# One layer of a hybrid encoder: the DeltaNet scan's q-k matrices as full 128x128 blocks, one product a step, and scratch buffers shared anew

## The chip, the cores and the metric

The kernel runs on one core of a Trainium2 chip. The metric is the time in microseconds (us) of one launch on that core; of several runs the median is taken, and the profile is of one execution. The core has engines that each work through a queue of their own, strictly in order: TensorE (PE: matrix products; PEld loads the stationary operand), VectorE (DVE), ScalarE (ACT), GpSimd (POOL) and SyncE (SP, which issues most transfers). Data lies in SBUF, products land in banks of PSUM, and semaphores make one engine wait for another.

## The reference, cut to what matters

768 tokens (one prompt of 256, one sample of 512), width 1024. The layer computes a modulated norm, one input projection, two mixers side by side (neighbourhood attention with 8 heads of 64; a gated DeltaNet in both directions with 4 heads of 128), one output projection, and a gated feed-forward part with a short convolution. The change is in the DeltaNet scan and in the norm of the attention's queries and keys:

```python
def _gated_delta_chunked(q, k, v, g, beta):          # CHUNK = 64
    ...
    a_mat = lower + jnp.eye(CHUNK, dtype=lower.dtype)
    u = lax.linalg.triangular_solve(a_mat, v * beta[..., None], ...)
    w = lax.linalg.triangular_solve(a_mat, kb * jnp.exp(gc)[..., None], ...)
    intra = jnp.where(causal, jnp.einsum('bhncd,bhnsd->bhncs', q, k) * decay, 0.0)
    ...
    def step(S, xs):
        q_i, k_i, u_i, w_i, a_i, gl_i = xs           # a_i is intra, the q-k matrix of a chunk
        v_new = u_i - jnp.einsum('bhcd,bhde->bhce', w_i, S)
        o = jnp.einsum('bhcd,bhde->bhce', q_i, S) + jnp.einsum('bhcs,bhse->bhce', a_i, v_new)
        S = S * jnp.exp(gl_i)[..., None, None] + jnp.einsum('bhcd,bhce->bhde', k_i, v_new)
        return S, o
...
    aq = _rmsnorm(aq.reshape(B, T, N_ATT_HEADS, ATT_HD), att_q_norm)
    ak = _rmsnorm(ak.reshape(B, T, N_ATT_HEADS, ATT_HD), att_k_norm)
```

## The kernel before, in words

**Tiling.** Weights and activations of the large projections are split into a high and a low half (hi, lo) and multiplied in three products (hi by hi, lo by hi, hi by lo); a projection is a long row of such products that depend on nothing but loaded weights. The DeltaNet's own products are plain 32-bit ones, each of which the trace shows as two instructions.

**The DeltaNet, by pairs of heads.** For each of two pairs (0 and 1) the stages are: `dn_proj` (q, k, v of the pair), `dn_decay`, `dn_scales`, `dn_gram` (the Gram products and from them `Ic`, the q-k matrices), `dn_solve` (the inverse of the triangular matrix of every chunk, a chain of small DVE and PE operations), `dn_scan`, and `dn_final` (squares on ACT L830, a Newton rsqrt of eleven small DVE operations L155 to L160 and L831, scaling on ACT L837, transposes on PE L842, gating on DVE L845, a store).

**A scan step.** A step handles one chunk of the forward direction in one half of the 128 partitions and one of the backward direction in the other. A scan has 24 steps: four rounds with both sequences and both heads of the pair (16 steps), and then four rounds with the sample alone (8 steps, two heads abreast). One step runs through this chain: the products of state and keys and queries (L768), `r` on DVE (two halves, L774) and `tm` on ACT (two halves, L781), the product with the inverse (L782), its scaled copies `XS` on DVE and ACT (L786, L788), two 64x128 copies into `XB` on ACT (L790), the products for the new state (L793), the state on DVE (two, L796), and the q-k products. `XB` holds each direction's rows with zeros in the other half, and two products with a 64-column operand (L802) give the two halves of the result, to which DVE adds `tm` (L806). The three groups of products of a step land in one PSUM bank. The state of the next step needs L796, so the rounds of one head and sequence follow each other.

**After a scan.** L818 adds the directions, and `dn_final` follows. After the second pair come the attention's blocks: `att_qk` projects 256 columns of queries or keys of half the heads (`att_proj`, L868), copies them to `raw` (L878), takes 24 squares with row sums on ACT into a throw-away tile `jk` (L884), forms the rsqrt on DVE (L885 and L155 to L160), multiplies (L888), and transposes on PE (L894). `att_v` projects the values, `att_core` does scores, softmax and mixing (first products at L944). The modulation vectors of the second norm are computed along the way (`ada`, L192).

**What sets the order.** The program text is not the order in which an engine works. A scheduler places the instructions of each engine; it may pull later, independent work, above all the projections, in between the steps of a scan. It can't pull a piece of work ahead of the last user of a buffer that it needs: every tile has a tag in a pool with a number of buffers, and the tiles of one tag take the buffers in turn, in the order of the program text. In the kernel before, `raw`, `jk` (tag `jka`), `s_` and `f_` of `att_qk` are in a pool `at` of their own, and `dn_final`'s `jk` is in the pool `dn` of the DeltaNet.

Of the kernel before, what the change touches and what calls it, by code (L numbers as in the profile page):

```python
# [17 lines left out]
P = 128  # L18
T = 768
D = 1024  # L20
# [25 lines left out]
NV1 = VEC["n1g"][0]  # L46
NC1 = CST["bo"][0]
# [55 lines left out]
def layer(ctx: ExitStack, tc: tile.TileContext, I: dict, yout: bass.AP, dbg=None):  # L103
# [7 lines left out]
    vec = cpool.tile([P, VEC["_n"][1] - NV1], F32, name="vec")  # L111
# [3 lines left out]
    nc.sync.dma_start(vec[:], I["vec"][:, NV1:])  # L115
    nc.scalar.dma_start(cst[:], I["cst"][:, NC2:])

    vec2 = []

    def V(n, i=0, m=None):  # L120
        o, w = VEC[n]
        t_, o = (vec, o - NV1) if o >= NV1 else (vec2[0], o)
        return t_[:, o + i:o + (i + m if m is not None else w)]
# [14 lines left out]
    def load_w(pool, src, bufs, hp=HPW):  # L138
        """[128, 1024] weights -> (hi, lo)"""
# [11 lines left out]
    def rsqrt(out, v, shape, tag):  # L151
        """out = v ** -0.5 (v > 0), Newton on the integer seed"""
        a = small.tile(shape, F32, name="rs_a", tag="rs_a" + tag, bufs=2)
        ti = small.tile(shape, I32, name="rs_t", tag="rs_t" + tag, bufs=2)
# [23 lines left out]
    bw = cpool.tile([P, KD, 32], F32R, name="bw")  # L178
    braw = arow[:, 0:128].rearrange("p (k c) -> p k c", k=KD)
    nc.scalar.dma_start(braw, I["wba"])  # L180
    split(braw, bw[:, :, 0:16], bw[:, :, 16:32])

# [4 lines left out]
    def ada_piece(s, i, row, brow, load, PS, w4=None):  # L187
        """rows k = 4 i.. of set s; the four partial sums in rows 32 k.."""
# [26 lines left out]
    def ada_ahead(sets, row, bias, load, PS):  # L215
        """each piece is loaded a step before it is used"""
# [24 lines left out]
    # ================= mixer =================  # L241
    with ExitStack() as mx:
# [20 lines left out]
        with tc.tile_pool(name="st", bufs=1, reuse_waits="tile") as st:  # L263
# [13 lines left out]
            # x, features on partitions  # L277
# [7 lines left out]
            # rstd of the tokens, along the free axis  # L285
# [50 lines left out]
            # the first four products run along with the rows of h  # L336
# [32 lines left out]
        at = px.enter_context(tc.tile_pool(name="at", bufs=1, side="right", reuse_waits="tile"))  # L369
# [14 lines left out]
        def gates_dn():  # L384
# [13 lines left out]
            ba = dn.tile([P, NT, 16], F32, name="ba")  # L398
# [3 lines left out]
            def to_slots(dst, src):  # L402
                """src [P, t, (d h)] -> dst [P, h, t', d]"""
# [10 lines left out]
            beta = dn.tile([P, 4, NT, 2], F32, name="beta")  # L414
            to_slots(beta, e1[:])
            y1 = dn.tile(sc8, F32, name="y1")
            nc.vector.tensor_tensor(y1[:], ba[:, :, 8:16], V("dtb").unsqueeze(1).broadcast_to(sc8), ALU.add)
            y2 = dn.tile(sc8, F32, name="y2")
# [4 lines left out]
            na = dn.tile([P, 8], F32, name="na")  # L423
            nc.scalar.activation(na[:], V("alog"), AF.Exp)
            nc.vector.scalar_tensor_tensor(y1[:], y1[:], -1.0, na[:].unsqueeze(1).broadcast_to(sc8), ALU.mult, ALU.mult)
            gg = dn.tile([P, 4, NT, 2], F32, name="gg")
# [16 lines left out]
            pdec = dn.tile(s48, F32, name="pdec")  # L443
# [40 lines left out]
        def ada_bufs():  # L484
            """buffers that the heads have left: five for weights, one for the bias row"""
# [3 lines left out]
            for tag, shape in (("dec", [P, 24, 64]), ("MO", [P, 12, P])):  # L489
                a_ = dn.tile(shape, F32, name="au", tag=tag)[:].rearrange("p a b -> p (a b)")  # L490
                raws.append(a_[:, 0:1024].rearrange("p (k c) -> p k c", k=2))
# [4 lines left out]
        def ada_load(src):  # L496
            """four k of a set"""
# [85 lines left out]
        def dn_scales(hp, sqs):  # L583
            # sums of squares: natural for k, swapped halves for q
# [6 lines left out]
            rkk = dn.tile([P, 2, NT], F32, name="rkk", tag="rkk", bufs=2)  # L591
# [782 lines left out]
```

## Time and profile before

| what | value |
|---|---|
| runs | 1201.08, 1195.68, 1190.89 us; median 1195.68 |
| span of the profiled execution | 1191.6 us |
| PE busy | 1150.3 us, 97% of the span |
| DVE / ACT / POOL busy | 726.8 us (61%) / 539.0 us (45%) / 69.0 us (6%) |
| scan of pair 0 | about 196 to 277 us of the span |
| solve of pair 1 | about 277 to 326 us |
| scan of pair 1 | about 326 to 407 us |
| first scores of the attention (L944) | 438.0 us |

The page gives no time around the span, so the profiled execution's own time is taken as its span; it lies 4.1 us, 0.3%, below the median of the runs and beside the fastest of them. A busy engine isn't one that sets the pace everywhere: what a stage is worth is read from that stage. In a row of a group, "x48 | 12.4, 259 | 2.3 <-PE" reads: 48 instructions, 12.4 us busy in all, 259 ns each in the mean, 2.3 us in which the engine stood idle before them, mostly waiting for PE.

### The profile page before, as it was taken

How to read it: one execution, taken by the hardware profiler on the slowest of the kernel's cores; microseconds unless marked ns; L12 is line 12 of the kernel's file. 1: busy time of each engine (PE TensorE's matmuls, PEld its weight loads, DVE VectorE, ACT ScalarE, POOL GpSimd, SP SyncE). 2: the span in 40 equal slices, each digit the busy share in tenths (PEclk: the TensorE clock that was granted, in tenths of full speed). 3: DMA queues.
4: the chain of work that ended last, by engine and by line, in shares of the span. 5: the costliest groups of instructions: out<-in, count | busy, mean ns of one | idle time of the engine just before them, and what ended most of it. 6: DMA issues, size and time to landing. Idle time of an engine off the chain costs nothing.

```text
span 1191.6 us, 17540 instructions
## 1 busy us (share of the span) xinstructions
PE 1150.3 (97%) x6682; PEld 940.3 (79%) x6682; DVE 726.8 (61%) x1544; ACT 539.0 (45%) x1301; POOL 69.0 (6%) x112
## 2 busy tenths in 40 slices
PE   6999899998999999999889999999999999999998
PEld 3778767777978698867678888888888888888886
DVE  5636986878476545364597655555655555564556
ACT  4357664574658666563476421430341233043310
POOL 1102103001100100100031000000000000000000
PEclk8999999999899999989999999999999999999999
DMA  8421142124241562281123411320311231031002
GB/s 306 197 71 36 54 142 90 58 94 142 73 149 55 176 231 72 76 264 60 59 75 106 142 54 29 113 66 6 115 63 36 71 89 53 18 102 58 19 1 106
DMA packets 43891, 110.98 MB, mean 93 GB/s; under 512 B 4384, under 2 KB 14528, under 8 KB 42528
## 3 DMA queue, kind: packets, MB, share of 16 engines
q1 hardware_dynamic: 36640, 92.93, 24.1%
q0 software_dynamic: 2928, 10.50, 2.7%
q10 hardware_dynamic: 4240, 6.44, 1.5%
q8 instruction: 52, 0.85, 0.3%
q14 instruction: 31, 0.25, 0.1%
HBM read 100.41 MB, written 9.45 MB: 92 GB/s over the span
## 4 chain that ended last, share of the span: by engine, by line
PE 79%; DVE 9%; ACT 7%; DMA 2%; issue 2%; SPq 0%; POOL 0%; DVEq 0%; ACTq 0%
PE dpt L1250 14%; PE upp L1169 10%; PE pjt L476 5%; PE pjt L868 4%; PE pat L1086 3%; PE sht L192 2%; PE pjt L345 2%; PE sdt L768 2%; ACT jk L884 1%; PE sdt L345 1%; PE sdt L944 1%; PE sdt L793 1%; PE sdt L802 1%; PE sdt L708 1%; PE mxt L970 1%
## 5 line engine op out<-in xcount | busy, mean ns | idle before, releaser
L136 DVE TENSOR_TENSOR wlo<-wraw,whi 128x1024 fp32r<-128x1024 f32 x72 | 88.1, 1223 | 115.9 <-ACT whi L135 115.7
L135 ACT CAST whi<-wraw 128x1024 fp32r<-128x1024 f32 x72 | 75.5, 1048 | 149.6 <-PE upp L1169 112.3
L1250 PE MATMUL dpt<-dh,gh 128*128 128x512 f32 x264 | 104.1, 395 | 0.2 <-DVE arow L1252 0.2
L1250 PE MATMUL dpt<-dl,gh 128*128 128x512 f32 x264 | 102.8, 389 | 0.0
L1250 PE MATMUL dpt<-dh,gl 128*128 128x512 f32 x264 | 102.3, 390 | 0.0
L1169 PE MATMUL upp<-h2lo,whi 128*128 128x256 f32 x352 | 99.8, 283 | 0.0
L1169 PE MATMUL upp<-h2hi,whi 128*128 128x256 f32 x352 | 98.8, 281 | 0.0
L1169 PE MATMUL upp<-h2hi,wlo 128*128 128x256 f32 x352 | 98.2, 279 | 0.0
L135 ACT CAST dh<-draw 128x1024 fp32r<-128x1024 f32 x22 | 23.1, 1052 | 160.4 <-PE dpt L1250 111.7
L1252 DVE TENSOR_TENSOR arow<-dpt,gb 128x512 f32<-128x512 f32 x72 | 49.8, 691 | 61.7 <-PE dpt L1250 59.6
L868 PE MATMUL pjt<-whi,hhi 128*128 128x256 f32 x288 | 85.4, 296 | 0.0
L868 PE MATMUL pjt<-whi,hlo 128*128 128x256 f32 x288 | 84.7, 294 | 0.0
L868 PE MATMUL pjt<-wlo,hhi 128*128 128x256 f32 x288 | 84.2, 292 | 0.0
L476 PE MATMUL pjt<-hhi,whi 128*128 128x512 f32 (+1 forms) x192 | 67.6, 352 | 1.3 <-DVE u L531 1.3
L476 PE MATMUL pjt<-hhi,wlo 128*128 128x512 f32 (+1 forms) x192 | 67.5, 353 | 0.0
L476 PE MATMUL pjt<-hlo,whi 128*128 128x512 f32 (+1 forms) x192 | 67.5, 352 | 0.0
L1169 PEld LDWEIGHTS upp<-h2hi,wlo 128*128 128x128 f32 x352 | 66.8, 190 | 0.2
L1169 PEld LDWEIGHTS upp<-h2hi,whi 128*128 128x128 f32 x352 | 66.3, 188 | 0.4
L1169 PEld LDWEIGHTS upp<-h2lo,whi 128*128 128x128 f32 x352 | 66.5, 189 | 0.0
L1250 PEld LDWEIGHTS dpt<-dh,gh 128*128 128x128 f32 x264 | 49.6, 188 | 13.4 <-DVE arow L1252 3.6
L868 PEld LDWEIGHTS pjt<-whi,hhi 128*128 128x128 f32 x288 | 55.9, 194 | 4.4 <-issue 3.6
L868 PEld LDWEIGHTS pjt<-whi,hlo 128*128 128x128 f32 x288 | 56.0, 195 | 2.5 <-issue 2.5
(910 smaller groups left out, 2882.7 us busy)
## 6 DMA issues: line engine op xcount, KB each, us to landing
wraw<-wup SPq DMA_DIRECT2D x44, 512.0 KB, 3.6
draw<-wdown SPq DMA_DIRECT2D x22, 512.0 KB, 3.5
araw<-ada SPq DMA_DIRECT2D x8, 1024.0 KB, 11.8
wraw<-wdn SPq DMA_DIRECT2D x16, 512.0 KB, 3.6
ew<-ada_w SPq DMA_DIRECT2D x16, 512.0 KB, 4.5
wraw<-wat SPq DMA_DIRECT2D x12, 512.0 KB, 4.1
sc<-abias POOLq DMA_DIRECT2D x24, 256.0 KB, 3.0
aw<-ada_w SPq DMA_DIRECT2D x10, 512.0 KB, 5.3
```

Source lines behind the costliest of these rows:

```text
L135: nc.scalar.copy(hi, src)
L136: nc.vector.tensor_tensor(lo, src, hi.bitcast(F32), ALU.subtract)
L192: nc.tensor.matmul(p_[32 * kk:32 * kk + 32, :], cs[:, 4 * i + kk, :], w4[kk], start=True, stop=True)
L345: nc.tensor.matmul(o_, w0[i][w][:, k * P:(k + 1) * P], m[:, k, c0:c1], start=(k == 0 and n == 0 and (c0 > 0 or i % 2 == 0)), stop=(k == KD ...
L476: nc.tensor.matmul(o_, w[:, k * P:(k + 1) * P], m[:, k, c0:c1], start=(k == 0 and n == 0), stop=(k == KD - 1 and n == 2))
L708: nc.tensor.matmul(ps[:, n * 32:n * 32 + 32], M16[:, n, :], R[:, n, :], start=True, stop=True)
L768: nc.tensor.matmul(ps1[:, d * P:(d + 1) * P], KQ[:, j, tl[d], 2 * pr[d]:2 * pr[d] + 2, :].rearrange("p b c -> p (b c)"), St[:, d, :], star ...
L868: nc.tensor.matmul(o_, a[:, k, t * P:(t + 1) * P], w[kh][m][:, kk * 256:(kk + 1) * 256], start=(k == 0 and n == 0 and t % 2 == 0), stop=(k ...
L1086: nc.tensor.matmul(pt[:], m[:, a, j, :], w[:, sl], start=(j == 0 and n == 0), stop=(j == len(ks) - 1 and n == 2))
L1169: nc.tensor.matmul(o_, (lo if n == 2 else hi)[:, k * P:(k + 1) * P], (h2lo if n == 1 else h2hi)[:, k, c0:c1], start=(k == 0 and n == 0), s ...
L1250: nc.tensor.matmul(ps[:], a[:, t * P:(t + 1) * P], m[:, sl], start=(i == 0 and n == 0), stop=(i == len(gs) - 1 and n == 2))
L1252: nc.vector.tensor_tensor(arow[:], ps[:], gb[:, grp(t), sl], ALU.mult)
```

## The change

**The q-k matrices.** `Ic` holds a full 128x128 block for every chunk instead of a 128x64 one. It is cleared on POOL, and the Gram stage writes each direction's 64x64 piece off the diagonal. `XB` and its clearing go. After the product with the inverse, ACT copies the whole 128x128 result once, back into `r` (which gets four buffers instead of two), and one product `Ic` by `r` gives both halves.

**The buffers.** `Ic` is larger by 12 KB a partition in two buffers, and other buffers are merged: the pool `at` goes. `rd` of `dn_decay`, which was in `at`, takes the tag `MO` of the solve. The attention's raw queries and keys lie in the second half of a buffer of tag `Ic` (`rest[0]`), whose first half holds the scores; both buffers are allocated before `att_half(0)`. `s_` and `f_` take the tags `beta` and `pdec`. The squares' throw-away tile `jk` of `att_qk` takes the tag `jk`, one buffer, which is also that of `dn_final`. The four states are one tile. Further small tiles share tags, three vectors at the end of `vec` are loaded later, by a POOL transfer in the output projection's phase, and some weights of the output projection are loaded into `rest[1]`.

```diff
-        XB = dn.tile([P, 2, 2, P], F32, name="XB", tag="XB")
-        nc.gpsimd.memset(XB[:], 0.0)
...
-            rd = at.tile([P, 24, 64], F32, name="rd", tag="raw")
+            rd = dn.tile([P, 24, 64], F32, name="rd", tag="MO")
...
-            Ic = dn.tile([P, 2, NT, 2, 64], F32, name="Ic", tag="Ic", bufs=2)
+            Ic = dn.tile([P, 2, NT, 2, P], F32, name="Ic", tag="Ic", bufs=2)
+            nc.gpsimd.memset(Ic[:].rearrange("p h t x c -> p (h t x c)"), 0.0)
...
-                            nc.vector.tensor_tensor(Ic[r_, j, b:b + n, e if d == 0 else 1 - e, :],
+                            nc.vector.tensor_tensor(Ic[r_, j, b:b + n, e if d == 0 else 1 - e, (1 - e) * 64:(1 - e) * 64 + 64],
...
-                r = dn.tile([P, P], F32, name="r", tag="r", bufs=2)
+                r = dn.tile([P, P], F32, name="r", tag="r", bufs=4)
...
-                for e in range(2):
-                    nc.scalar.copy(xb[half(e), e, :], ps2[half(e)])
+                nc.scalar.copy(r[:], ps2)
...
-                for e in range(2):
-                    nc.tensor.matmul(ps4[half(1 - e)], Ic[:, j, tp, x, :], xb[:, e, :], start=True, stop=True)
+                nc.tensor.matmul(ps4, Ic[:, j, tp, x, :], r[:], start=True, stop=True)
...
-            raw = at.tile([P, NT, 4, 64], F32, name="raw", tag="raw", bufs=1)
+            raw = rest[0].rearrange("p (t h c) -> p t h c", t=NT, h=4)
...
-            s_ = at.tile([P, 24], F32, name="s_", tag="s_")
-            f_ = at.tile([P, 24], F32, name="f_", tag="f_")
+            s_ = dn.tile([P, 24], F32, name="s_", tag="beta")
+            f_ = dn.tile([P, 24], F32, name="f_", tag="pdec")
             for i in range(24):
-                jk = at.tile([P, 64], F32, name="jk", tag="jka", bufs=1)
+                jk = dn.tile([P, 64], F32, name="jk", tag="jk", bufs=1)
                 nc.scalar.activation(jk[:], raw[:, i // 4, i % 4, :], AF.Square, accum_out=s_[:, i:i + 1])
...
+        scs, rest = [], []
+        for i in range(2):
+            sc3 = dn.tile([P, 6, 512], F32, name="sc", tag="Ic", bufs=2)
+            scs.extend(sc3[:, u] for u in range(3))
+            rest.append(sc3[:, 3:6].rearrange("p a b -> p (a b)"))
...
-                raw = wo.tile([P, D], F32, name="wraw", tag="wraw", bufs=WRB)[:]
+                raw = wo.tile([P, D], F32, name="wraw", tag="wraw")[:] if i % 2 else rest[1][:, 0:D]
...
+        vec3.append(fp.tile([P, VEC["_n"][1] - NV2], F32, name="vec3"))
+        nc.gpsimd.dma_start(vec3[0][:], I["vec"][:, NV2:])
```

**How the order changes.** In the changed file the lines carry slightly other numbers: its L769, L783, L801, L841, L867, L883, L893 and L191 are L768, L782, L802, L842, L868, L884, L894 and L192 of before. On PE, the last rounds of the second pair's scan in the kernel before: `pjt` is a projection's PSUM tile, `au`, `aw` and `arow` are operands of the modulation, `sdt` the scan's tile.

```order
L768 MATMUL sdt<-S_2915,KQ 128x128
L192 MATMUL sht<-au,cs 32x512 x3
L192 MATMUL sht<-aw,cs 32x512
L782 MATMUL sdt<-r,Wbd 128x128
L192 MATMUL sht<-aw,cs 32x512 x3
L868 MATMUL pjt<-whi,hhi 128x256
L868 MATMUL pjt<-whi,hlo 128x256
L868 MATMUL pjt<-wlo,hhi 128x256
L782 MATMUL sdt<-r,Wbd 128x128
L802 MATMUL sdt<-XB,Ic 64x128 x2
```

The same place in the changed kernel, up to the first projection after the scan:

```order
L769 MATMUL sdt<-S,KQ 128x128
L801 MATMUL sdt<-r,Ic 128x128
L769 MATMUL sdt<-S,KQ 128x128 x2
L783 MATMUL sdt<-r,Wbd 128x128 x2
L801 MATMUL sdt<-r,Ic 128x128 x2
L841 MATMUL sdt<-cst,Vt 128x128 x12
L893 MATMUL sht<-cst,sc 128x128 x12
L191 MATMUL sht<-aw,cs 32x512 x6
L191 MATMUL sht<-au,cs 32x512 x2
L867 MATMUL pjt<-whi,hhi 128x256
```

Projection and modulation products no longer stand between these rounds. In the changed kernel this holds for the last 15 of the scan's 24 steps, and the twelve transposes of `dn_final` (L841) and the first twelve of the raw queries (L893) stand ahead of the next projection product; in the kernel before the transposes L842 stand one by one between L868's.

On ACT, in the middle of the second pair's scan in the kernel before; the squares of the raw keys (into `s__3911`) stand between the scan's copies:

```order
L884 ACTIVATE jk,s__3911<-raw 128x64 x2
L790 COPY XB<-sdt 64x128 x2
L781 ACTIVATE tm<-sdt,egcs 64x128 x2
L830 ACTIVATE jk,so<-Vt 128x128
L884 ACTIVATE jk,s__3911<-raw 128x64
```

On ACT, at the end of the same scan in the changed kernel:

```order
L782 ACTIVATE tm<-sdt,egcs 64x128 x4
L790 COPY r<-sdt 128x128 x2
L829 ACTIVATE jk,so<-Vt 128x128 x10
L883 ACTIVATE jk,s__3524<-sc 128x64 x7
L836 ACTIVATE Vt<-Vt,fo 128x128 x11
L846 DMA mixn_73<-zz 128x768
L836 ACTIVATE Vt<-Vt,fo 128x128
L883 ACTIVATE jk,s__3524<-sc 128x64 x4
L846 DMA mixn_73<-zz 128x768
L883 ACTIVATE jk,s__3524<-sc 128x64 x13
```

All 24 squares of the first raw queries (`s__3524`) now stand behind the whole scan and behind `dn_final`'s squares (L829), two of which stand within the scan; in the kernel before all but one of the queries' squares stand ahead of the second pair's scan.

More of the change, by code (lines that the diff above doesn't have):

```diff
@@ L488, in ada_bufs @@
             raws.extend(w_[:, i] for i in range(3))
-            for tag, shape in (("dec", [P, 24, 64]), ("MO", [P, 12, P])):
-                a_ = dn.tile(shape, F32, name="au", tag=tag)[:].rearrange("p a b -> p (a b)")
+            for tag in ("dec", "MO"):
+                a_ = dn.tile([P, 1536], F32, name="au", tag=tag)
                 raws.append(a_[:, 0:1024].rearrange("p (k c) -> p k c", k=2))
@@ L747, in dn_scan @@
         def dn_scan(hp, KQ, Kt, Vt, pex, Ic, Wbd):
-            S = [[dn.tile([P, 2, P], F32, name=f"S{s}{j}", tag=f"S{s}{j}") for j in range(2)] for s in range(2)]
+            S_ = dn.tile([P, 4, 2, P], F32, name="S", tag="S")
+            S = [[S_[:, 2 * s + j] for j in range(2)] for s in range(2)]
             half = lambda e: slice(e * 64, e * 64 + 64)
@@ L886, in att_qk @@
             rsqrt(f_[:], s_[:], [P, 24], "24")
-            r3 = raw[:].rearrange("p t h c -> p (t h) c")
+            r3 = rest[0].rearrange("p (n c) -> p n c", c=64)
             nc.vector.tensor_tensor(r3, r3, f_[:].unsqueeze(2).broadcast_to([P, 24, 64]), ALU.mult)
@@ L1031, in layer @@
         att_half(0, iter(()), (0, 0, 0))
-        pTs = [dn.tile([P, 512], F32, name="pT", tag=t)[:] for t in ("XS", "XB")]
-        scs = []
-        for _ in range(2):
-            sc3 = dn.tile([P, 3, 512], F32, name="sc", tag="Ic", bufs=2)
-            scs.extend(sc3[:, u] for u in range(3))
+        pTs = [dn.tile([P, 512], F32, name="pT", tag=t)[:] for t in ("XS", "S")]
         core = att_core(0, QT[0], SD, SD, [(a, b, u) for a in range(2) for b in range(2) for u in range(3)])
@@ L1203, in out_proj @@
                 if t > 1:
-                    raw = wo.tile([P, KD, P], F32, name="mraw", tag="wraw", bufs=WRB)
+                    raw = (wo, wm)[t % 2].tile([P, KD, P], F32, name="mraw", tag="wraw")
                     m_ = wm.tile([P, 2, KD, P], F32R, name="m_", tag="m_", bufs=2)
```

43 lines of the change are left out of this document (21 added, 22 removed).

## The prediction

> **What bounds the kernel now.** First the page's head and its chain of waits, which say what the whole is limited by.
>
> ```profile
> span 1191.6 us, 17540 instructions
> PE 1150.3 (97%) x6682; PEld 940.3 (79%) x6682; DVE 726.8 (61%) x1544; ACT 539.0 (45%) x1301; POOL 69.0 (6%) x112
> PE 79%; DVE 9%; ACT 7%; DMA 2%; issue 2%; SPq 0%; POOL 0%; DVEq 0%; ACTq 0%
> ```
>
> PE is busy for 97% of the span and carries 79% of the chain that ends last. So an instruction taken off PE is worth its time there, and time in which PE stands still is lost in full, unless the span has such time already. The second view is therefore the busy time by stage: solve of the second pair, its scan, the stretch up to the first scores (columns: span of time, its length, busy of PE, PEld, DVE, ACT and POOL with counts, granted clock, DMA share, GB/s).
>
> ```profile
> 277.00:326.00 49.00, 43.49 (x317) 41.95 (x317) 28.84 (x64) 28.53 (x104) 4.99 (x8) 0.90 0.34 115
> 326.00:407.00 81.00, 79.76 (x578) 58.95 (x576) 54.70 (x162) 52.83 (x184) 1.16 (x4) 1.00 0.32 105
> 407.00:438.00 31.00, 31.00 (x246) 27.13 (x245) 11.42 (x30) 17.77 (x66) 3.71 (x7) 1.00 0.89 300
> ```
>
> The scan is a chain through three engines, yet PE idles 1.24 us of 81 in it and nothing in the 31 us after it: independent projection products fill what the scan's waits leave. Whatever takes this filling away turns the chain's waits into PE time.
>
> **The products: what goes from PE.** A scan step has six products at two instructions each; the pair of L802 is two 64-column ones. PE's own rows in the first scan, in order of time (start, duration, name, count):
>
> ```profile
> 212.63 0.40 PE L476 MATMUL pjt<-hlo,whi 128*128 128x512 f32 x1
> 212.86 0.61 PE L793 MATMUL sdt<-XS,Kt 128*128 128x128 f32 x4
> 213.31 0.39 PE L782 MATMUL sdt<-r,Wbd 128*128 128x128 f32 x2
> ...
> 214.47 0.28 PE L476 MATMUL pjt<-hhi,whi 128*128 128x256 f32 x1
> 214.68 0.44 PE L802 MATMUL sdt<-XB,Ic 128*64 128x128 f32 x4
> 215.04 0.39 PE L476 MATMUL pjt<-hlo,whi 128*128 128x256 f32 x1
> 215.27 0.28 PE L476 MATMUL pjt<-hhi,wlo 128*128 128x256 f32 x1
> 215.38 0.29 PE L476 MATMUL pjt<-hhi,whi 128*128 128x256 f32 x1
> 215.51 0.28 PE L476 MATMUL pjt<-hlo,whi 128*128 128x256 f32 x1
> 215.63 0.61 PE L768 MATMUL sdt<-S,KQ 128*128 128x128 f32 x4
> 215.99 0.36 PE L476 MATMUL pjt<-hhi,wlo 128*128 128x256 f32 x1
> 216.19 0.28 PE L476 MATMUL pjt<-hhi,whi 128*128 128x256 f32 x1
> ```
>
> Durations overlap, so I go by starts. A projection product of 256 columns takes 0.12 us (215.27 to 215.51 holds two). From 214.47 to 215.27 stand the L802 pair and two of those: 0.80 - 0.24 = 0.56 us for the pair. From 215.51 to 216.19 stand two full products of L768 and two of those: 0.68 - 0.24 = 0.44, 0.22 for one. A step saves 0.34 us, 48 steps 16.3 us. The bounds: by durations alone, 0.44 for L802 against 0.39 for the one product L782, it is 0.05 a step, 2.4 us; were L782's 0.14 us to the next start the price of one product, it is 0.42, 20 us. I take 16, since it sets groups with the same neighbours against each other.
>
> By the Trainium skill's page TensorEngine Tiling (Array Packing), Key Properties, separate tiles of the array work in parallel, while changing the tiling mode drains it. By the first half of this alone a pair would cost no more than one full product and the sum would be 16 us higher; the pair's 0.56 us against 0.22 bears out the second half.
>
> **The copies.** Two ACT copies become one of 128x128; the nearest row of that size is L804.
>
> ```profile
> L790 ACT COPY XB<-sdt 64x128 f32<-64x128 f32 x48 | 12.4, 259 | 2.3 <-PE sdt L782 1.1 <-PE sdt L802 0.6
> L804 ACT COPY Wbd<-sdt 128x128 f32<-128x128 f32 x4 | 1.1, 264 | 1.3 <-PE sdt L802 1.2
> ```
>
> That takes 48 times 0.25, 12 us, off ACT, which is 45% busy: nothing while PE is filled, and 0.25 us of a round where it isn't (counted below).
>
> **The order: what moves.** The squares of the first raw queries share one buffer with `dn_final`'s squares, and the buffer goes round in the order of the text. So they stand on ACT behind the whole second scan. Until they are done `raw` can't be rewritten, the projection's PSUM tiles aren't freed, and neither the next attention blocks nor the modulation products that stand behind them on PE can be placed. The order rows show the consequence: the last 15 of the 24 steps have nothing between their products, and the projections follow after `dn_final`'s and the queries' transposes. The work itself isn't lost; it stood before these steps or follows them. What it loses is its cover: for each stretch I compare PE's work with what the other engines need.
>
> *Seven steps with both sequences.* DVE's rows of the second scan:
>
> ```profile
> L774 DVE SCALAR_TENSOR_TENSOR r<-sdt,negc,Vt 64x128 f32<-64x128 f32 x40 | 13.9, 348 | 2.5 <-PE sdt L768 1.1
> L796 DVE SCALAR_TENSOR_TENSOR S<-S,egl,sdt 128x128 f32<-128x128 f32 x32 | 9.7, 343 | 8.3 <-PE sdt L793 5.6 <-ACT XB L790 1.2 <-ACT raw L878 1.0
> L806 DVE TENSOR_TENSOR Wbd<-sdt,tm 128x128 f32<-128x128 f32 x20 | 5.8, 292 | 6.8 <-PE sdt L802 6.5
> L786 DVE TENSOR_TENSOR XS<-sdt,pex 64x128 f32<-64x128 f32 x20 | 5.7, 287 | 5.2 <-PE sdt L793 2.5 <-PE sdt L782 2.2
> L818 DVE TENSOR_TENSOR Vt<-Wbd 64x512 f32<-64x512 f32 x4 | 2.7, 684 | 0.1
> ```
>
> A step costs DVE two L774, one L786, two L796 (9.7 over 32, 0.30 each, since they overlap) and one L806: 0.70 + 0.29 + 0.60 + 0.29 = 1.88 us. PE needs 12 instructions at 0.11 (L793 above: four from 212.86 to 213.31), 1.32 us. Four streams are enough to hide the latencies, so DVE sets the pace: 7 times 0.56, 4 us idle, 5 with some handover.
>
> *Four rounds with two heads.* Now a round is a chain. For each head pair of a round ACT has these rows:
>
> ```profile
> L781 ACT ACTIVATE tm<-sdt,egcs 64x128 f32<-64x128 f32 x40 | 14.5, 363 | 7.3 <-DVE r L774 3.4 <-DVE Wbd L806 2.3 <-DVE rs_a L158 0.6
> L788 ACT ACTIVATE XS<-sdt,pex 64x128 f32<-64x128 f32 x20 | 7.2, 361 | 12.1 <-DVE XS L786 12.0
> ```
>
> L768 0.61, two L774 0.70, two L781 on the same bank 0.73, L782 0.39, L786 0.29, L788 0.36, the copy 0.26, L793 0.61, two L796 0.60: 4.55 us, and some nine handovers, which I put at 0.12 each (an estimate; no row isolates one): 5.6 us a round. PE works 2 times 1.32 = 2.64 in it; idle 3.0, four times, 12 us. The bounds: half, if the two heads overlap better than I think, since DVE alone needs 3.8 us a round (1.2 idle, 5 us in all); 18 if handovers cost twice as much.
>
> *The tail behind the scan.* ACT and DVE in the same place of before:
>
> ```profile
> 412.05 0.31 ACT L830 ACTIVATE jk<-Vt 128x128 f32<-128x128 f32 x1
> 412.48 0.31 ACT L830 ACTIVATE jk<-Vt 128x128 f32<-128x128 f32 x1
> 420.56 3.33 ACT L837 ACTIVATE Vt<-Vt,fo 128x128 f32<-128x128 f32 x11 [0.96 <-DVE fo L160]
> 432.32 0.59 ACT L878 COPY raw<-pjt 128x512 f32<-128x512 f32 x1 [1.95 <-PE pjt L868]
> 432.94 0.26 ACT L884 ACTIVATE jk<-raw 128x64 f32<-128x64 f32 x1
> 433.32 0.26 ACT L884 ACTIVATE jk<-raw 128x64 f32<-128x64 f32 x1
> ```
>
> The last L806 and L818 cost about 0.3 + 3 × 0.68 = 2.3 us before the squares can run freely. Then ACT, by its order: 10 squares of `dn_final` at 0.43 (412.05 to 412.48) 4.3; 7 of the queries at 0.38 2.7, which cover the rsqrt on DVE; the scaling 3.3 + 0.4; two stores that ACT issues and that wait for the gating, about 0.7; 17 squares more at 0.38, 6.5. Then DVE:
>
> ```profile
> 447.26 0.18 DVE L885 TENSOR_SCALAR s__4398<-s__4398 128x24 f32<-128x24 f32 x1 [0.56 <-ACT jk L884]
> 449.86 1.76 DVE L888 TENSOR_TENSOR raw<-raw,f__4399 128x1536 f32<-128x1536 f32 x1
> ```
>
> 2.6 us from L885 to L888, and 1.76. In all 2.3 + 4.3 + 2.7 + 3.7 + 0.7 + 6.5 + 4.4 = 24.6, with handovers 25.5. In it PE has 12 transposes, some 2.6 us: 23 us idle. ACT's serial work alone is 17 us, so it can't be under 15; 27 if the stores wait long.
>
> *The keys.* The queries' turn is followed by the keys': three copies, 24 squares, 4.4 on DVE, about 17 us (3 × 0.59, 24 × 0.4, 4.4 and handovers). Against it the order leaves about 80 projection products at 0.12 and 16 of modulation, twice as wide, at 0.24: 13.5 us of cover. So 3 us, between 0 and 6.
>
> **The clock.** In the solve's stretch:
>
> ```profile
> 290.00:310.00 20.00, 16.25 (x100) 15.87 (x98) 9.67 (x15) 10.43 (x32) 2.15 (x2) 0.74 0.10 28
> ```
>
> A mean of 0.74 over 20 us is about 10 us at half rate, behind 3.75 us without PE work. The tail is a longer gap than that. If it ends in such a stretch, 10 us of filled PE give half their work, 5 us; most of it may be spent on the transposes and the modulation products. I take 4, from 0 to 10. The Trainium skill's page TensorE: Matmul & The Clock Gate, Part 1, names half rate after an idle window of about 3.4 us; by it this change pays for its gaps twice, and the row agrees.
>
> **The rest.** The fill that stood in the second scan partly stands ahead of the first (6 to 7 us more, by the order's rows counted out at these prices), so that scan starts later and is shorter; the second pair's solve then lies wholly behind it with less cover: 3 us (0 to 6), against the 5.5 us that PE idles there now. The two clearings of `Ic` are twice the size of this one of `MO`; behind it a table load on ACT:
>
> ```profile
> 106.33 1.38 POOL L657 MEMSET MO<- 128x1536 f32 x1 [62.82 <-PE sht L438]
> ...
> 208.30 1.28 ACT L629 ACT_TABLE_LOAD   x1
> ```
>
> 2.8 us each; by the order they lie in such idle POOL time, and without that the Gram stage would wait 2.8. `rd` in `MO` waits for the first solve, done long before. Two table loads more on ACT (1.28 us each) and the late `vec3` lie beside PE work. SP's weight load for the output projection stands early and holds up modulation weights that are used much later: nothing. From the first scores on, PE's order is that of before.
>
> **The sum.** Of the 112 us from the second scan's start to L944, about 6 are stalls already (1.24 idle, and products that start late), which the new idle time replaces. So: -16 products, +5 +12 +23 +3 = +43 new idle, -6 old, +2 for stalls in the nine steps that stay filled, +3 solve, +4 clock: +30. 1191.6 + 30 = 1222 for the profiled execution; the median lies 0.3% above that span, which I don't add, since the fastest run lies at it.
>
> **The rivals.**
>
> *The waits only eat the gain.* The rounds overlap (5 instead of 12), the tail takes its floor of 15, the clock doesn't drop: 5 + 5 + 15 + 0 idle, -6 + 2, -16: about 1197. For it: a floor of a serial chain is what I reckoned from durations with handovers only estimated. Against: L788 waits 12 us for L786 in 20 steps even now, so the chain is as serial as I take it. Chance 0.19.
>
> *Half products cost much more than 0.34 a step, and it gets faster.* The mechanism is the emptying of the array before and after every L802 pair, in all 48 steps. It decides from 46 / 48 = 0.96 us a step, where it pays for all the idle time; at 1.2 a step the time is 1180. For it: L802's neighbours, too, start late (0.36 us from 214.68 to 215.04). Against: a filled scan takes 81 us for 24 steps, 3.4 a step, with six products and two to three projection products of each step in it; what isn't explained there is 6 us, 0.27 a step, so that the most is 0.6. Chance 0.08.
>
> *The pair costs nothing more than one product* (the parallel tiles): the same waits and no saving, 1238. Against it stands 0.56 to 0.22. Chance 0.05.
>
> *PE stays at half rate* through the rounds and the tail: 2.64 us a round become 5.3, of which half lies in the chain, and the seven steps become PE-bound; with the transposes some 15 us more, 1237. For it: 3 us of idle time in each round; against: the work between them. Chance 0.10.
>
> My forecast: 0.58.
>
> **How the numbers follow.** A measurement of this kernel can tell about 1% from no change, 12 us. The forecast lies 2.2% above the median of 1195.68. Slower by over 1% (above 1207.6): 0.58 + 0.05 + 0.10 = 0.73; within 1%: 0.19; faster: 0.08. The range runs from 1197, the first rival's time, to 1240, the two slow ones': that leaves out the faster one and half of the first, under 0.2.
>
> **What would show it.** In the changed profile: L802's successor with two instructions a step; a second scan with PE busy well under 9 tenths in its latter part; some 20 us without PE work between the last q-k product and the queries' transposes, ended by DVE's L888; a granted clock under 1 about there; the stretch from the first scores on as long as before. I am wrong if PE is 9 tenths busy through the scan's end, or if the tail is under 12 us.

## The result, and the profile after

The changed kernel takes 1230.07 us (median of four runs, 1228.87 to 1231.62) against 1194.18 for the kernel before: a ratio of 1.0296, 95% interval 1.0263 to 1.0330. It is slower by 3%. The forecast was 1222, range 1197 to 1240. Two further series gave 1.0280 (1.0266 to 1.0294) and 1.0273 (1.0246 to 1.0300).

The page of the changed kernel, its head and the busy times:

```profile
span 1226.6 us, 17311 instructions
...
PE 1151.0 (94%) x6586; PEld 950.2 (77%) x6586; DVE 728.7 (59%) x1544; ACT 529.7 (43%) x1255; POOL 70.2 (6%) x114
```

96 instructions of PE are gone, but its busy time is as before (1151.0 against 1150.3; part of it now runs at half rate and so counts longer), and the time without PE work has grown from 41.3 to 75.6 us. Where, the view of busy time by stretch shows: the first nine steps of the second scan, its next seven, three of the last four rounds, the fourth, the tail up to the queries' transposes, the stretch up to the first projection product, and the way to the first scores (columns as in the prediction; the third number from the end is the granted clock).

```profile
326.00:349.30 23.30, 23.24 (x182) 21.81 (x181) 14.88 (x46) 11.62 (x36) 0.00 (x0) 1.00 0.24 91
349.30:366.00 16.70, 12.51 (x68) 9.78 (x67) 11.91 (x37) 9.50 (x29) 0.00 (x0) 0.92 0.09 32
366.00:372.80 6.80, 5.10 (x26) 4.53 (x25) 3.77 (x13) 2.71 (x8) 0.00 (x0) 0.75 0.00 1
372.80:379.30 6.50, 4.99 (x26) 4.37 (x25) 3.64 (x13) 2.48 (x8) 0.00 (x0) 0.76 0.01 3
379.30:386.20 6.90, 5.23 (x26) 4.62 (x25) 3.83 (x13) 2.71 (x8) 0.00 (x0) 0.75 0.00 0
386.20:390.90 4.70, 3.37 (x17) 2.55 (x16) 2.24 (x8) 1.98 (x6) 0.00 (x0) 0.86 0.00 0
390.90:414.80 23.90, 3.87 (x12) 2.18 (x12) 11.90 (x38) 15.90 (x80) 3.18 (x6) 0.50 0.45 154
414.80:421.80 7.00, 6.16 (x28) 2.71 (x28) 3.76 (x5) 4.56 (x21) 0.00 (x0) 0.53 0.02 2
421.80:471.50 49.70, 49.01 (x360) 38.27 (x356) 12.37 (x23) 21.10 (x77) 0.53 (x1) 1.00 0.69 233
```

PE is busy for 23.24 of 23.30 us in the nine filled steps, for 31.2 of the following 41.6 us, and for 3.87 of 23.90 in the tail. The second scan starts at 326.3 us (before: 326.0), the first scores at 471.5 (before: 438.0), and from there to the end it is 755.1 us (before: 753.6). So 33 of the 35 us lie between the second scan's start and the first scores, in the place that the order had shown.

The tail itself, PE in order of time (in brackets the idle time before an instruction, and who ended it):

```profile
389.84 1.06 PE L801 MATMUL sdt<-r,Ic 128*128 128x128 f32 x4
399.99 3.40 PE L841 MATMUL sdt<-cst,Vt 128*128 128x128 f32 x11 [9.09 <-ACT Vt L836]
403.70 0.47 PE L841 MATMUL sdt<-cst,Vt 128*128 128x128 f32 x1 [0.31 <-ACT Vt L836]
414.83 1.97 PE L893 MATMUL sht<-cst,sc 128*128 128x128 f32 x8 [10.66 <-DVE sc L887]
417.61 1.12 PE L893 MATMUL sht<-cst,sc 128*128 128x128 f32 x4 [0.80 <-DVE QT L907]
418.65 2.77 PE L191 MATMUL sht<-aw,cs 128*32 128x512 f32 x10
...
421.83 0.39 PE L867 MATMUL pjt<-whi,hhi 128*128 128x256 f32 x1
```

PE stands still for 9.09 us, until ACT has scaled the outputs, and for 10.66 us, until DVE has multiplied the raw queries. On ACT and DVE the links of this chain are the ones that the forecast had added up:

```profile
392.68 0.31 ACT L829 ACTIVATE jk<-Vt 128x128 f32<-128x128 f32 x1 [2.37 <-DVE Vt L817]
...
397.01 0.26 ACT L883 ACTIVATE jk<-sc 128x64 f32<-128x64 f32 x1
...
399.55 3.31 ACT L836 ACTIVATE Vt<-Vt,fo 128x128 f32<-128x128 f32 x11
...
410.05 0.26 ACT L883 ACTIVATE jk<-sc 128x64 f32<-128x64 f32 x1
```

```profile
413.02 1.76 DVE L887 TENSOR_TENSOR sc<-sc,f__3525 128x1536 f32<-128x1536 f32 x1
```

### The profile page after: what moved, and what is told of

Read it like the earlier page. It is cut to its first block, busy times and chain, and to the rows that moved or that the text cites. A ratio compares the mean times of both kernels' runs of the same rounds, so it can differ in the third digit from the quotient of the medians.

```text
span 1226.6 us, 17311 instructions
## 1 busy us (share of the span) xinstructions
PE 1151.0 (94%) x6586; PEld 950.2 (77%) x6586; DVE 728.7 (59%) x1544; ACT 529.7 (43%) x1255; POOL 70.2 (6%) x114
## 4 chain that ended last, share of the span: by engine, by line
PE 75%; DVE 9%; ACT 9%; DMA 3%; issue 3%; SPq 0%; ACTq 0%; POOL 0%; DVEq 0%
PE dpt L1253 13%; PE upp L1172 10%; PE pjt L867 4%; PE pjt L475 3%; PE pat L1087 3%; PE sdt L793 2%; PE pjt L344 2%; ACT jk L883 2%; PE sht L191 1%; PE sdt L344 1%; PE sdt L943 1%; PE dpt L1087 1%; PE sdt L769 1%; PE sdt L783 1%; PE sdt L709 1%
## 5 line engine op out<-in xcount | busy, mean ns | idle before, releaser
L867 PE MATMUL pjt<-whi,hhi 128*128 128x256 f32 x288 | 84.6, 294 | 0.0
L867 PE MATMUL pjt<-wlo,hhi 128*128 128x256 f32 x288 | 83.7, 291 | 0.0
L867 PE MATMUL pjt<-whi,hlo 128*128 128x256 f32 x288 | 83.5, 290 | 0.0
L867 PEld LDWEIGHTS pjt<-whi,hhi 128*128 128x128 f32 x288 | 56.2, 195 | 4.8 <-issue 3.5
L1253 PEld LDWEIGHTS dpt<-dh,gl 128*128 128x128 f32 x264 | 49.6, 188 | 10.5
```

The costliest lines, as they stand in the source:

```text
L867: nc.tensor.matmul(o_, a[:, k, t * P:(t + 1) * P], w[kh][m][:, kk * 256:(kk + 1) * 256], start=(k == 0 and n == 0 and t % 2 == 0), stop=(k ...
L1253: nc.tensor.matmul(ps[:], a[:, t * P:(t + 1) * P], m[:, sl], start=(i == 0 and n == 0), stop=(i == len(gs) - 1 and n == 2))
```

## The experiments

The theory to be tested: the shared one-buffer `jk` takes the projections out of the second scan, which costs some 46 us, and the full blocks give some 16 back. The rival: the larger blocks, their clearing and the other merged buffers cost the time, and `jk` is beside the point.

**Own buffer for `jk`.** In the changed kernel `dn_final`'s squares go to the buffers of tag `r`, so that the attention's squares have `jk` for themselves.

```diff
 def dn_final
-                    jk = dn.tile([P, P], F32, name="jk", tag="jk", bufs=1)
+                    jk = dn.tile([P, P], F32, name="jk", tag="r", bufs=4)
```

> The changed kernel with dn_final's throw-away squares in the buffers of tag r, so that jk of the attention's squares no longer waits for them; all else as changed. By the forecast's theory (the lost cover of the second scan is what costs) the projections return between the scan's steps, the tail of 24 us and the half-rate clock go, and the products' saving of 16 us shows: about 1178 us (1172 to 1186), faster than before by over 1%. If the products save nothing: about 1192. By the rival that the larger q-k blocks, their clearing and the other merged buffers are what costs, it stays above 1215.

Measured: 1186.71 us, ratio to the kernel before 0.9937 (0.9920 to 0.9954); a second series 1187.91, 0.9939 (0.9924 to 0.9954). Against the changed kernel (1230.07 and 1229.19) the tag of a tile that nobody reads is worth 41 to 43 us, and without the sharing the change is a gain. It beats the kernel before too, but by 7 to 8 us and not by 16, a little outside the 1172 to 1186 that were expected. Its page, and the stretch of its second scan:

```profile
PE 1140.1 (96%) x6586; PEld 941.2 (79%) x6586; DVE 726.2 (61%) x1544; ACT 526.2 (44%) x1255; POOL 69.7 (6%) x114
```

```profile
325.00:402.00 77.00, 76.57 (x546) 60.68 (x545) 56.44 (x167) 47.12 (x162) 1.30 (x3) 1.00 0.39 126
```

The scan is filled again (76.57 of 77.00), the clock is 1.00.

**The shared `jk` alone.** The kernel before with this one edit:

```diff
 def att_qk
-                jk = at.tile([P, 64], F32, name="jk", tag="jka", bufs=1)
+                jk = dn.tile([P, 64], F32, name="jk", tag="jk", bufs=1)
```

> The kernel before with one edit alone: jk of the attention's squares takes the tag jk of dn_final. By the forecast's theory the second scan loses its cover as in the changed kernel, while the half products stay: about 1236 us (1230 to 1244). By the rival that the new blocks and the other merged buffers cost the time, it stays at 1192.

Measured: 1237.04 us, ratio 1.0371 (1.0334 to 1.0407), 42 us slower. The rival falls: without any larger block the same loss appears.

**Half products in the changed kernel's buffers**, with and without the shared `jk`. `Ic` uses half of its large buffer, and `XB` lies in the rest of it:

```diff
-            Ic = dn.tile([P, 2, NT, 2, P], F32, name="Ic", tag="Ic", bufs=2)
-            nc.gpsimd.memset(Ic[:]..., 0.0)
+            I_ = dn.tile([P, 3072], F32, name="Ic", tag="Ic", bufs=2)
+            nc.gpsimd.memset(I_[:, 1536:2048], 0.0)          # XB
+            Ic = I_[:, 0:1536]...
...
-                nc.scalar.copy(r[:], ps2)
+                for e in range(2):
+                    nc.scalar.copy(xb[half(e), e, :], ps2[half(e)])
...
-                nc.tensor.matmul(ps4, Ic[:, j, tp, x, :], r[:], start=True, stop=True)
+                for e in range(2):
+                    nc.tensor.matmul(ps4[half(1 - e)], Ic[:, j, tp, x, :], xb[:, e, :], start=True, stop=True)
```

> As the first run here, but with two 64-column products and two half copies a step as before (64-column q-k matrices and XB in the large buffer). Its distance to the first run is the price of the half products with their copies in a filled scan: 16 us by the row of the forecast (0.34 us in 48 steps), so about 1193; 0 to 2 us if two tiles of the array run as one, so about 1180; its distance to the kernel before is what the other merged buffers cost, by the forecast nothing (0 to 6).

> The changed kernel, shared jk kept, with two 64-column products and two half copies a step as before. By the forecast the saving is 0.34 us a step where PE is filled (about 31 steps) and smaller in the uncovered steps, where a second copy and a second product lengthen little of the chain: 11 to 16 us slower than the changed kernel, about 1238. If the half products cost nothing: 1227.

Measured: with its own `jk` 1196.14 us, ratio 1.0025 (1.0004 to 1.0047); with the shared one 1240.47, ratio 1.0399 (1.0358 to 1.0439). The four kernels in the changed buffers make a square:

| | own `jk` | shared `jk` | difference |
|---|---|---|---|
| two half products | 1196.14 | 1240.47 | 44.3 |
| one full product | 1186.71 | 1230.07 | 43.4 |
| difference | 9.4 | 10.4 | |

The two edits add up as far as these runs can tell: the interval of the slowest kernel's ratio is 5 us either way, and the 1230.07 are of the earlier series. The full product is worth 9.4 us in a filled scan, 0.20 us a step, and not 16; in the uncovered scan it is 10.4, just under the 11 to 16 that were expected. The remaining merged buffers, with `XB` in the large one, cost 3 us (0.25%, between 0.04 and 0.47).

**Products or copies.** To see whether PE or the second ACT copy makes the 9.4 us, the kernel with its own `jk` takes two 64-column products out of the full block and the same `r`, with one copy:

```diff
-                nc.tensor.matmul(ps4, Ic[:, j, tp, x, :], r[:], start=True, stop=True)
+                for e in range(2):
+                    nc.tensor.matmul(ps4[half(1 - e)], Ic[:, j, tp, x, (1 - e) * 64:(1 - e) * 64 + 64], r[:], start=True, stop=True)
```

> The first run's kernel (own buffer for jk, full blocks, one copy), but the q-k product taken as two 64-column products out of the same full block and the same r; nothing else differs. It parts the 9.4 us between the half products with two copies and the full product with one. If the products' price on PE is the whole of it: 9 to 10 us slower than the first run, about 1196. If the second copy on ACT is what costs: 0 to 2 us slower, about 1187. By the forecast's price of 0.34 us a step: 16 us slower, 1203.

And the same kernel with the full product issued twice:

```diff
                 nc.tensor.matmul(ps4, Ic[:, j, tp, x, :], r[:], start=True, stop=True)
+                nc.tensor.matmul(ps4, Ic[:, j, tp, x, :], r[:], start=True, stop=True)
```

> The first run's kernel with the full q-k product issued twice, one right behind the other, into the same place; the second result replaces the first and is the same. It prices a full product that has a neighbour of its own kind: by the forecast's row 0.22 us each, 10.6 us in 48 steps, about 1197. If only the first of a group is dear and a pass behind its like costs 0.11 us, the same 10.6 us; if a product alone costs 0.30 us each time, 14 us, about 1201.

The kernel with its own `jk`, again, beside them:

> The first run's kernel again, on this chip beside the others, as the base of their differences: 1184 to 1189 us.

Measured: two products 1197.95 us, 10.0 above the 1187.91 of the base; twice the full one 1195.64, 7.7 above. So the split of the product alone makes up the 9.4 us, and no price of the copy shows beside it, as the forecast had it for filled PE. A split costs 0.21 us a step more than one product. A second full product right behind the first costs 0.16 by the medians, less than any of the three expectations; but the runs with it spread from 1194.18 to 1201.73, by their mean it is 0.18, and the expected 0.22 isn't clearly excluded.

**The tail apart from the scan.** Of the kernel with its own `jk`, the first keys' squares alone go to the buffers of tag `r`, which scan and `dn_final` use, and so behind the scan:

```diff
 def att_qk
-                jk = dn.tile([P, 64], F32, name="jk", tag="jk", bufs=1)
+                jk = (dn.tile([P, 64], F32, name="jk", tag="r", bufs=4) if (hf, which) == (0, 1)
+                      else dn.tile([P, 64], F32, name="jk", tag="jk", bufs=1))
```

> The first run's kernel with jk of the first keys alone put behind the second scan (in the buffers of tag r, which scan and dn_final use), while the first queries' jk stays free. By the order the scan's steps are filled again to the end, and only the tail behind the scan stays without projections, but for some twenty. It parts the two stretches of the forecast: the tail's 23 us less 3 us of cover, with some 3 us of half-rate clock, so about 20 to 24 us above the first run, 1207 to 1211. If the uncovered steps in the scan were nearly all of the loss: 1190 to 1195; if the tail were all of it: 1225 to 1230.

Measured: 1213.13 us, ratio 1.0143 (1.0111 to 1.0174), 25.2 above its base, just over the 20 to 24 that were expected. Its PE at the end of the second scan, the last filling product and what follows:

```profile
396.57 0.28 PE L867 MATMUL pjt<-wlo,hhi 128*128 128x256 f32 x1
402.99 3.40 PE L841 MATMUL sdt<-cst,Vt 128*128 128x128 f32 x11 [6.14 <-ACT Vt L836]
406.73 0.48 PE L841 MATMUL sdt<-cst,Vt 128*128 128x128 f32 x1 [0.33 <-ACT Vt L836]
414.97 1.97 PE L893 MATMUL sht<-cst,sc 128*128 128x128 f32 x8 [7.77 <-DVE sc L887]
```

The tail is there, 14.2 us idle, with filled steps ahead of it. So of the 41.3 us between the changed kernel (1229.19) and its own-`jk` form (1187.91), about 25 belong to the tail and its clock, about 16 to the 15 uncovered steps. This split is rough: the interval of the ratio is some 4 us either way, and this tail isn't quite the changed kernel's, where PE stands still for 20.1 us. Nor is all of the 25 accounted for. By the pages of the profile PE's time without work grows by 15.5 us over the base (58.8 against 43.3); the rest is longer PE time for the same 6586 instructions, of which the half rate from 400.94 to 421.42 us, with 9.30 us of PE work in it, explains about half.

**The clock behind the tail.** In the changed kernel, products whose results nobody reads run on PE in the tail: first 64 columns wide, behind each of the queries' squares, behind the scaling of the sums and behind the rsqrt.

```diff
 def att_qk (only for hf == 0 and which == 0)
+            wr = lambda i, v: nc.tensor.matmul(warm[:, 0:64], raw[:, i // 4, 0:2, :]..., v[:, i:i + 1].broadcast_to([P, 64]), start=True, stop=True)
             for i in range(24):
                 nc.scalar.activation(jk[:], raw[:, i // 4, i % 4, :], AF.Square, accum_out=s_[:, i:i + 1])
+                wr(i, s_)
...
+            for i in range(10): wr(i, s_)          # behind the scaling of s_
             rsqrt(f_[:], s_[:], [P, 24], "24")
+            for i in range(8): wr(i, f_)
```

> The changed kernel with throw-away products on PE in the tail: behind each of the first queries' 24 squares, behind their sum's scaling and behind the rsqrt, a 64-column product whose result nobody reads. PE then works in the tail's second half, where it stood still. The rate of the clock is the only thing that this can better. If half rate behind the gap costs what the trace shows (about 415 to 421.5 us at half), the transposes and the modulation products run at full rate and it gains 3 to 4 us, about 1226 to 1227 beside 1230. If the clock costs nothing there: 1230 to 1232 (the dummies delay the transposes by up to 1 us).

> The changed kernel again, on the same chip as the run with the throw-away products, as its base: 1228 to 1232 us.

Measured: 1238.86 us (ratio 1.0368, 1.0354 to 1.0382), beside 1229.19 for the changed kernel; 10 us slower instead of 3 faster. Two of its rows, the stretch with the dummies and the transposes behind it:

```profile
402.00:421.00 19.00, 18.61 (x87) 18.23 (x86) 3.35 (x16) 6.21 (x35) 0.00 (x0) 0.50 0.11 43
423.00:427.00 4.00, 3.15 (x16) 2.29 (x20) 1.94 (x4) 1.39 (x4) 0.00 (x0) 0.50 0.00 0
```

PE is shown busy for 18.61 of 19 us, yet the clock stays at 0.50 all through and behind it. The dummies do no good, and they harm: DVE's multiplication of `raw` has to wait until they have read it (5.65 us). So this run doesn't price the clock.

The second form is wider: 256 columns, a fixed matrix in `raw`'s place, and none ahead of the last stores.

```diff
 def att_qk (only for hf == 0 and which == 0)
+            wr = lambda i, v: nc.tensor.matmul(warm[:, 0:256], ident, v[:, i:i + 1].broadcast_to([P, 256]), start=True, stop=True)
...
+                if 11 <= i < 23: wr(i, s_)
...
+            for i in range(7): wr(i, s_)
             rsqrt(f_[:], s_[:], [P, 24], "24")
+            for i in range(6): wr(i, f_)
```

> The changed kernel with denser throw-away products in the last part of the tail: 256 columns wide, a fixed matrix as the stationary operand, 12 of them behind the first queries' last squares, 7 behind the scaling of the sums and 6 behind the rsqrt; nobody reads the results. If work on PE of this density brings the granted clock back within some 3 us, as the 512-column products of the modulation do in the changed kernel, the transposes and the work behind them run at full rate: 3 us faster than the changed kernel, about 1226. If the clock stays at half as with the 64-column dummies: 0 to 3 us slower than the changed kernel, 1229 to 1233.

> The changed kernel again as the base of the run with denser throw-away products: 1228 to 1232 us.

Measured: 1232.87 us (1.0314, 1.0285 to 1.0343), beside 1228.66. The stretch in which its dummies begin, the end of the dummies, and what stands behind them:

```profile
409.80:414.50 4.70, 4.62 (x11) 3.72 (x12) 0.00 (x0) 4.21 (x25) 0.00 (x0) 0.50 0.21 85
...
424.00:429.00 5.00, 3.93 (x30) 1.51 (x28) 3.67 (x5) 3.24 (x13) 0.00 (x0) 1.00 0.07 9
```

```profile
418.09 0.18 DVE L889 TENSOR_SCALAR s__3524<-s__3524 128x24 f32<-128x24 f32 x1 [9.01 <-PE sdt L887]
```

These do bring the clock back: it is at 1.00 from about 415.2 us on, 5.3 us after the first dummy (409.88). The way from the first queries' transpose to the first projection product then takes 5.0 us (424.08 to 429.05) instead of the 7.0 of the changed kernel (414.83 to 421.83): 2.0 us is the price of half rate behind the tail. The whole is no faster, since the dummies at half rate pile up and DVE's scaling waits for them until 418.09: 24.2 us behind the start of the last q-k products (393.88), where in the changed kernel it is 20.6 (389.84 to 410.44). The mechanism shows in the stretch; a remedy it isn't.

## Why the prediction was right, and which terms were not

The direction, the place and the mechanism held: the loss sits between the second scan's start and the first scores, comes with the shared `jk` and goes with it. The time came out 8 us above the forecast. 2 to 3 of these are no term of the sum: the later runs show that a profiled execution's own time lies 1.9 to 3.0 us above its span, so the span of 1191.6 stood for about 1194, and the forecast should have been read as 1224. Term by term:

- *Products, "A step saves 0.34 us, 48 steps 16.3 us"*: this is the step that failed. Measured 9.4 and 10.0, 0.20 to 0.21 us a step. The forecast had priced every pair like one that stands alone between projection products. PE's rows show how that can go wrong: of the 24 pairs in the second scan before, only five stand between projection products, and the others have products of the scan, of the modulation or transposes beside them. Two steps' pairs side by side in the kernel before:

```profile
366.24 0.28 PE L868 MATMUL pjt<-wlo,hhi 128*128 128x256 f32 x1
366.44 0.66 PE L802 MATMUL sdt<-XB,Ic 128*64 128x128 f32 x8
367.03 0.39 PE L868 MATMUL pjt<-whi,hhi 128*128 128x256 f32 x1
367.25 0.28 PE L868 MATMUL pjt<-whi,hlo 128*128 128x256 f32 x1
```

  From 366.24 to 367.25, less 0.24: 0.77 us for two pairs, 0.39 each instead of 0.56. And a full product standing alone between projection products, in the kernel with its own `jk`:

```profile
346.53 0.28 PE L867 MATMUL pjt<-whi,hlo 128*128 128x256 f32 x1
346.65 0.38 PE L801 MATMUL sdt<-r,Ic 128*128 128x128 f32 x2
346.78 0.36 PE L867 MATMUL pjt<-wlo,hhi 128*128 128x256 f32 x1
346.99 0.28 PE L867 MATMUL pjt<-whi,hhi 128*128 128x256 f32 x1
```

  From 346.53 to 346.99, less 0.24, it is 0.22 us, the forecast's price. In that scan seven full products stand so: four take 0.22 us, three 0.38 to 0.48. The single pairs before take 0.56, 0.56 and 0.76, so that between projection products the rows still give about the forecast's 0.34; the difference must lie in the other places, and that they make all of it is argued and not shown. The run with both products is what counts: 0.21.
- *Tail, 23 us, and the clock's 4*: measured idle 9.09 + 0.31 + 10.66 = 20.1 us, and 23.9 us from the last q-k product's sum to the transposes against 25.5 reckoned. Of the 1.6 us by which the chain is shorter, 0.6 is its start (ACT's squares begin 1.74 us after the sum does, not 2.3) and the rest mostly the handovers; ACT's waits at the stores, 0.39 and 0.47, came out about as reckoned (0.7). PE's idle time is less by 1.3 more because the twelve transposes ran at half rate (3.87 us instead of 2.6). With the keys and the clock about 25 by the run that has the tail alone (roughly, see there), against 23 + 3 + 4.
- *Seven steps, 5, and four rounds, 12*: 16.7 us for the seven against 14.2 reckoned, 24.9 for the four against 22.4; by the runs roughly 16 us of loss for all 15. PE stands still for 4.2 us in the seven, as reckoned, but for 6.2 in the four rounds (24.9 less 18.7 busy) and not for 12; the rest of the rounds' loss is longer PE time. The rounds take 6.5 to 6.9 us instead of 5.6. In one of them PE shows why:

```profile
373.65 0.61 PE L769 MATMUL sdt<-S,KQ 128*128 128x128 f32 x4
375.32 0.49 PE L783 MATMUL sdt<-r,Wbd 128*128 128x128 f32 x2 [1.07 <-ACT tm L782]
376.09 0.49 PE L783 MATMUL sdt<-r,Wbd 128*128 128x128 f32 x2 [0.28 <-ACT tm L782]
376.74 1.99 PE L793 MATMUL sdt<-XS,Kt 128*128 128x128 f32 x8 [0.17 <-ACT r L790]
378.52 0.63 PE L769 MATMUL sdt<-S,KQ 128*128 128x128 f32 x2
```

  The eight instructions of L793 take 1.78 us to the next start, 0.22 each, twice the 0.11 of before: they run at half rate, some 0.9 us in a chain that the forecast had reckoned at full rate.
- *Clock*: I had expected half rate from the end of the tail on. It began 50 us earlier, in the last rounds (0.75 in the mean), and cost 2.0 us behind the tail and about 0.9 us in a round. The rival "PE stays at half rate" was thus partly what happened, but only partly: in the rounds the clock comes back each time.
- *Solve, 3 us*: not seen by itself. The second scan starts at 326.3 instead of 326.0 us; how the first scan's saving, the fill pulled ahead of it and the solve share in that, no run parts. The remaining buffers' 3 us, which the run with half products shows, were put at nothing; where they arise wasn't tried.
- *From the first scores on*: 755.1 against 753.6 us, as forecast but for 1.5.

Added up by runs that don't contain the changed kernel itself: 42 for the shared `jk` (the kernel before with that one edit), 3 for the merged buffers, -9.4 for the products: 36, against a measured 33 to 36 (the three series). In the forecast two terms were too large, the gain by 7 and the loss of cover by 3 to 5. They have opposite signs, so its sum came closer than its parts; that much of the hit is luck. The rivals: that the waits only eat the gain (1197) falls, since the tail took nearly its reckoned length, 20.1 us of idle time, and not its floor of 15, and the four rounds took 24.9 us, more than the 22.4 reckoned. That half products cost 0.96 us a step or more falls with 0.20. That the pair costs no more than one product falls, too: the measured 0.21 us a step lies between "tiles run in parallel" and the forecast's price. By the Trainium skill's page TensorEngine Tiling (Array Packing), Key Properties, a change of the tiling mode drains the engine; the lower price of the two neighbouring pairs, 0.39 against 0.56 in one place, agrees with a cost per change of mode and not per product.

## What to carry to other kernels

A scratch tile that nobody reads still orders the program: with one buffer, its users stand in a row, and an early, independent piece of work that shares it with a late one can't be pulled ahead any more. Before buffers are merged to make room, see that the work that gives cover doesn't share with something late: here it was enough to move the late squares of `dn_final` to other buffers. Sharing with something early instead should do as well, but was not tried. And price an instruction by a run that has one more or one less of it: the rows of a few places gave 0.34 us where the run gave 0.20.

## What the runs showed of the hardware that was not expected

**The clock falls without a long gap.** In the last rounds of the changed kernel no gap on PE is longer than 1.14 us, and yet the granted clock goes to half and back in stretches of about 3.4 us. Six stretches in order of time:

```profile
360.00:363.00 3.00, 1.60 (x11) 1.12 (x9) 2.52 (x8) 2.79 (x11) 0.00 (x0) 1.00 0.00 0
364.00:366.50 2.50, 2.50 (x14) 2.50 (x13) 1.42 (x5) 0.13 (x1) 0.00 (x0) 0.50 0.00 0
367.00:370.00 3.00, 1.43 (x9) 0.85 (x7) 1.79 (x7) 2.00 (x6) 0.00 (x0) 1.00 0.01 3
371.00:373.00 2.00, 2.00 (x11) 2.00 (x11) 1.21 (x4) 0.00 (x0) 0.00 (x0) 0.50 0.00 0
374.00:377.00 3.00, 1.49 (x9) 0.92 (x8) 1.70 (x6) 2.02 (x7) 0.00 (x0) 1.00 0.00 0
377.50:380.00 2.50, 2.50 (x13) 2.50 (x12) 1.51 (x5) 0.00 (x0) 0.00 (x0) 0.50 0.03 7
```

Behind 3 us in which PE is busy for half of the time (1.60, 1.43, 1.49 us) stands a stretch at 0.50, and behind a full one a stretch at 1.00. It happens to fall in time with the rounds, so that the quick rate meets the waits and the half rate meets the products. The Trainium skill's page TensorE: Matmul & The Clock Gate, Part 1, speaks of an idle window of about 3.4 us; the length agrees, but here the window wasn't idle.

The share of busy time alone doesn't decide it, though. In the changed kernel these two stretches have the same share, and the clock falls behind the first only; behind the second it stays at 1.00 for another 3.3 us, in which PE does almost nothing:

```profile
359.95:363.35 3.40, 1.95 (x12) 1.28 (x10) 2.63 (x9) 3.03 (x11) 0.00 (x0) 1.00 0.00 0
...
291.70:295.10 3.40, 1.96 (x17) 1.75 (x15) 3.37 (x5) 1.66 (x6) 0.00 (x0) 1.00 0.44 124
295.10:298.40 3.30, 0.07 (x1) 0.10 (x1) 3.15 (x4) 2.94 (x7) 0.00 (x0) 1.00 0.08 31
```

The first holds the scan's 128-column products, the second 256-column products of a projection. And in the kernel before, the clock falls behind a stretch in which PE is busy all the time:

```profile
181.50:184.90 3.40, 3.40 (x32) 3.40 (x32) 1.50 (x8) 0.00 (x0) 1.05 (x2) 1.00 0.61 190
185.00:188.20 3.20, 3.20 (x13) 2.81 (x12) 2.57 (x7) 1.52 (x2) 1.13 (x1) 0.50 0.00 0
```

Nearly all of that full stretch are products of 32 columns (L708) and of 2 columns (L205).

**Busy isn't always enough to bring it back.** 19 us of 64-column products with hardly a gap (18.61 busy) left the clock at 0.50, while 256-column products brought it back 5.3 us after the first of them. What counts seems to be how much is streamed through the array and not that an instruction is shown as running. The two runs also differ in the matrix that is held; the stretches above point the same way, but no run varies the width alone, and it stays an inference.
